# A gate builder copies eight tokens at a time out of PSUM, and the sample's second top-k becomes background work

## The chip, the cores and the metric

The kernel runs on one core of a Trainium2 chip. The metric is the time of one execution on the device, in microseconds; a kernel's figure is the median of several runs. Five engines work side by side: TensorE (PE in the profile, with PEld for its weight loads), VectorE (DVE), ScalarE (ACT), GpSimd (POOL), and SyncE (SP), which here only issues transfers. Each engine works through its own instructions strictly in the order in which the program was built.

## The reference

One layer of a decoder for 512 prompt tokens and a sample of 64 tokens: attention beside a short convolution, and then PEER, a mixture of 16384 experts of one neuron each. PEER is what the change touches:

```python
s = jnp.einsum('nhpc,hpkc->nhpk', q, sub_keys)
sv, si = lax.top_k(s, PEER_TOPK)                 # first top-k: 16 of 128 keys, for 2 halves of 8 heads
cand = sv[:, :, 0, :, None] + sv[:, :, 1, None, :]
cid = si[:, :, 0, :, None] * PEER_NKEYS + si[:, :, 1, None, :]
top, pos = lax.top_k(cand, PEER_TOPK)            # second top-k: 16 experts for each head
eid = jnp.take_along_axis(cid, pos, axis=-1)
g = jax.nn.softmax(top, axis=-1)
act = jax.nn.gelu(jnp.einsum('nd,nhkd->nhk', xf, u[eid]), approximate=False)
out = jnp.einsum('nhk,nhkd->nd', g * act, v[eid])
```

So each token takes 128 (expert, gate) pairs.

## The kernel before

The tokens lie in blocks of 128: block 0 to 3 are the prompt, block 4 is the sample (64 rows). PEER is computed in two ways.

**Gathered**, for block 0 and block 4: GpSimd fetches one row of u for each token and slot (`row`, L469, 512 KB), VectorE takes the dot product with the token (L477); later the same with rows of v, which VectorE adds up (`accg`, L484 and L487). These gathers are handed out a few at a time by `pump`, between other work, from a list `bg` of generators; `left` is the estimate of what remains, from which the pace of the last loop (`tail`) is set.

**Dense**, for blocks 1 to 3 (384 tokens): all 16384 experts are worked out for all tokens in 128 chunks of 128 experts. A *u-step* (`ustep`) loads a chunk of u (`ur`), splits it on ScalarE into a high part `uh` (L103) and on VectorE into a low part `ul` (L104), runs 24 matmuls of 384 columns into `pu`, and ScalarE writes `a` = gelu (L782). A *v-step* (`vprep`, `vmm`) multiplies `a` by the gates of this chunk (`w`, L898), splits, and runs 18 matmuls of 512 columns into the accumulators `y`. The u-steps of the first 68 chunks (LAG) may run ahead of everything; their results wait in DRAM (`Ad`) or in SBUF. The v-loop then takes chunks 68 to 127 first, each with its u-step, and after that chunks 0 to 67.

Between them stands the **gate build** (`gbuild`), which turns the 128 (expert, gate) pairs of every dense token into a full row of 16384 gates. For eight tokens at a time (TQ, called a *unit* here; 48 units in all) VectorE writes three one-hot tiles (L844, and L848 twice: `oj`, `oi`), ScalarE a fourth by eight scaled copies (`oi`, L852), TensorE multiplies them token by token into `pG`, and ScalarE copies `pG` into the staging tile `stg`. Four units fill one `stg`, which goes to DRAM (`Gd`, 12 stores of 2 MB); the v-steps read it back (`gt`). In `stg` the token is the innermost index ([expert row, 128, 32 tokens]), in `pG` it is the outer one:

```python
pg_ = psG.tile([P, 4, P], F32, name="pG")
...
nc.scalar.activation(stg[:, :, tl:tl + 4].rearrange("p i t -> p t i"), pg_, AF.Copy, scale=1.0 / GSC)
```

So this copy reads 512 consecutive words of PSUM and writes each of them 128 bytes behind the last.

A v-step needs gates of all 384 tokens, so the first v-step waits for the last store of `Gd`. The program's order on every engine is set at build time by a scheduler with its own estimate of costs; it moves u-steps, gathers and the pieces of a second top-k (`topk2`) to where it thinks their inputs are ready. The second top-k of the sample (`topk_gather` with st, 4, 64) is called behind the gate build, in one piece.

Of the kernel before, what the change touches and what calls it, by code (L numbers as in the profile page):

```python
# [9 lines left out]
F32 = mybir.dt.float32  # L10
# [5 lines left out]
AF = mybir.ActivationFunctionType  # L16
# [3 lines left out]
P = 128  # L20
# [10 lines left out]
SLOTS = 128  # L31
# [24 lines left out]
TQ = 8  # L56
NTB = ND // TB
GSC = 16384.0
# [9 lines left out]
def body(tc, I, O):  # L68
    nc = tc.nc
    top = ExitStack()  # L70

    def pool(stack, name, bufs=1, **kw):
        return stack.enter_context(tc.tile_pool(name=name, bufs=bufs, reuse_waits="tile", **kw))
# [369 lines left out]
    bg = []  # L443

    credit = [0.0]
    left = [0.0]
# [13 lines left out]
    def drain(gen):  # L460
        for _ in gen:
            pass

    def gather_units(k, nslot):
        idx, gat, x2, acc, av = idxg[k], gatg[k], x2g[k], accg[k], avg[k]

        def row(src, s):
            r = rows.tile([P, D], F32, name="row")
            nc.gpsimd.indirect_dma_start(out=r, out_offset=None, in_=I[src],  # L469
                                         in_offset=bass.IndirectOffsetOnAxis(ap=idx[:, s:s + 1], axis=0))  # L470
            return r

        for s in range(nslot):
            r = row("u", s)
            jk = keep2.tile([P, D], mybir.dt.bfloat16, name="jk2")
            tc.keep_in_program_order(
                nc.vector.tensor_tensor_reduce(jk, r, x2, 1.0, 0.0, OP.mult, OP.add, av[:, s:s + 1]))  # L477
            yield 1.135
        nc.scalar.activation(av[:, :nslot], av[:, :nslot], AF.Gelu)
        nc.vector.tensor_tensor(av[:, :nslot], av[:, :nslot], gat[:, :nslot], op=OP.mult)  # L480
        for s in range(nslot):
            r = row("v", s)
            if s == 0:
                tc.keep_in_program_order(nc.vector.tensor_scalar(acc, r, av[:, 0:1], None, op0=OP.mult))  # L484
            else:
                tc.keep_in_program_order(
                    nc.vector.scalar_tensor_tensor(acc, r, av[:, s:s + 1], acc, op0=OP.mult, op1=OP.add))  # L487
            yield 1.135
# [70 lines left out]
    def topk_gather(st, b, n, k):  # L559
        ef = tk.tile([P, SLOTS], F32, name="ef", bufs=2)  # L560
        if n == P:
            yield from topk2(st, b, n, ef, gatg[k])
            nc.vector.tensor_copy(idxg[k], ef)
            return
        gt = tk.tile([P, SLOTS], F32, name="gt", bufs=2)
        ei = tk.tile([P, SLOTS], I32, name="ei")
        yield from topk2(st, b, n, ef, gt)
        hs = SLOTS // 2
        nc.vector.tensor_copy(ei[:n], ef[:n])
        nc.vector.tensor_copy(idxg[k][:n, :hs], ef[:n, :hs])  # L570
        nc.vector.tensor_copy(gatg[k][:n, :hs], gt[:n, :hs])
        nc.sync.dma_start(idxg[k][n:2 * n, :hs], ei[:n, hs:])
        nc.sync.dma_start(gatg[k][n:2 * n, :hs], gt[:n, hs:])
        nc.sync.dma_start(x2g[k][n:2 * n, :], x2g[k][:n, :])
# [139 lines left out]
    def mkst(pl, grp):  # L714
        return {b: (pl.tile([P, 8, 2, 16], F32, name=f"sv{b}"), pl.tile([P, 8, 2, 16], U32, name=f"si{b}"))
                for b in grp}
# [37 lines left out]
    st = mkst(x2p, GB)  # L754
# [34 lines left out]
    def unext():  # L789
        if ui[0] < LAG:  # L790
            ustep(ui[0])
            ui[0] += 1
            pump(PUMP_WIN)
# [9 lines left out]
    psG = pool(gb_, "psG", bufs=2, space=PSUM)  # L803
# [8 lines left out]
    def gbuild(di, b):  # L812
        ef = tk.tile([P, SLOTS], F32, name="ef", bufs=2)
        gt = tk.tile([P, SLOTS], F32, name="gt", bufs=2)
        yield from topk2(st, b, P, ef, gt)
        ei = tk.tile([P, SLOTS], I32, name="ei")
        ii = tk.tile([P, SLOTS], I32, name="ii")
        ij = tk.tile([P, 2, SLOTS], F32, name="ij")
        nc.vector.tensor_copy(ei, ef)
        nc.vector.tensor_scalar(ii, ei, 7, None, op0=OP.logical_shift_right)  # L820
        nc.vector.tensor_copy(ij[:, 0, :], ii)
        nc.vector.tensor_scalar(ii, ei, 127, None, op0=OP.bitwise_and)
        nc.vector.tensor_copy(ij[:, 1, :], ii)
        pt = psG.tile([P, 4, P], F32, name="pT")
        nc.tensor.transpose(pt[:, 0, :], ij[:, 0, :], ident)
        nc.tensor.transpose(pt[:, 1, :], ij[:, 1, :], ident)
        nc.tensor.transpose(pt[:, 2, :], gt, ident)
        JT = gbp.tile([P, P], F16, name="JT")
        J4 = gbp.tile([P, 2, P, 4], F16, name="J4")
        gs = gbp.tile([P, P], F32, name="gs", bufs=1)  # L830
        gl = gbp.tile([P, P], F32, name="gl")
        nc.vector.tensor_copy(JT, pt[:, 1, :])
        nc.vector.tensor_copy(J4[:, 0], pt[:, 0, :].unsqueeze(2).to_broadcast([P, P, 4]))
        nc.vector.tensor_scalar(gs, pt[:, 2, :], GSC, None, op0=OP.mult)
        nc.vector.tensor_copy(J4[:, 1], gs.unsqueeze(2).to_broadcast([P, P, 4]))
        nc.vector.tensor_tensor(gl, gs, J4[:, 1, :, 0], op=OP.subtract)
        yield 1.5
        for tb in range(P // TB):
            stg = gbp.tile([P, NCH, TB], F32, name="stg")
            for q in range(TB // TQ):  # L840
                c0 = tb * TB + q * TQ
                cs = slice(c0, c0 + TQ)
                oj = gbp.tile([P, P, TQ], F16, name="oj")
                nc.vector.tensor_tensor(oj, iotaj, JT[:, cs].unsqueeze(1).to_broadcast([P, P, TQ]), op=OP.is_equal)  # L844
                OI = [gbp.tile([P, 32, TQ, 4], F16, name=f"oi{k}") for k in range(3)]
                f = "p a t b -> p a (t b)"
                for k, in0, op in ((0, iotax, OP.is_equal), (1, OI[0], OP.mult)):
                    nc.vector.tensor_tensor(OI[k].rearrange(f), in0.rearrange(f),  # L848
                                            J4[:, k, cs, :].rearrange("p t b -> p (t b)").unsqueeze(1)
                                            .to_broadcast([P, 32, TQ * 4]), op=op)  # L850
                for tt in range(TQ):
                    nc.scalar.activation(OI[2][:, :, tt, :], OI[0][:, :, tt, :], AF.Copy, scale=gl[:, c0 + tt:c0 + tt + 1])  # L852
                for q4 in range(TQ // 4):
                    pg_ = psG.tile([P, 4, P], F32, name="pG")
                    for t in range(4):
                        tt = q4 * 4 + t
                        nc.tensor.matmul(pg_[:, t, :], oj[:, :, tt], OI[1][:, :, tt, :], start=True, stop=False)
                        nc.tensor.matmul(pg_[:, t, :], oj[:, :, tt], OI[2][:, :, tt, :], start=False, stop=True)
                    tl = q * TQ + q4 * 4
                    nc.scalar.activation(stg[:, :, tl:tl + 4].rearrange("p i t -> p t i"), pg_, AF.Copy,  # L860
                                         scale=1.0 / GSC)
                yield 2.5
            nc.sync.dma_start(Gd[di * (P // TB) + tb], stg)

    debt = 0.0
    for di, b in enumerate(DENSE):
        for c in gbuild(di, b):
            debt += c
            while debt > WSTEP:
                unext()  # L870
                debt -= WSTEP
    while ui[0] < LAG:
        unext()
    drain(topk_gather(st, 4, 64, 1))
    bg.append(gather_units(1, SLOTS // 2))
    left[0] += SLOTS * 1.135
    gb_.close()

    vp = pool(top, "vp", bufs=2)
# [155 lines left out]
```

## Time and profile before

| | before |
|---|---|
| median of 3 runs | 1884.6 us (1877.14 to 1884.9) |
| span of the profiled execution, first to last instruction | 1882.2 us |
| PE busy in the span | 1738.2 us (92%) |
| DVE busy | 1430.9 us (76%) |
| ACT busy | 881.6 us (47%) |
| mean granted TensorE clock | 0.955 |
| moved by DMA | 533.75 MB, mean 284 GB/s |

The time listed for the runs is that of whole executions; the profile shows one execution, whose span lies 2.4 us below the median. Busy times are unions of the instructions' intervals; an instruction's own duration is longer than the step to the next one where the two overlap.

### The profile page before, as it was taken

Reading aid. Unit: us, or ns where it says so; the run is one execution under the profiler, and the core shown is the slowest. Engines: PE = TensorE matmul, PEld = TensorE weight load, DVE = VectorE, ACT = ScalarE, POOL = GpSimd, SP = SyncE. Lnnn points to the kernel's source line nnn. Section 1 sums busy time; section 2 is a strip of 40 time slices with the busy share of each in tenths; the row PEclk is TensorE's granted clock in tenths of the full one; section 3 lists DMA queues with packets and bytes.
Section 4 is the critical chain, followed back from the end, with each engine's and each line's share of the span. In section 5 each row is a group of like instructions: output and inputs, shape, how many; then the busy total and the mean of one; then the engine's idle time right before and its main releaser. Section 6 shows DMA issues by size and latency. Waiting matters only on the chain. (4 is left out here: it accounts for less than half of the span.)

```text
span 1882.2 us, 29066 instructions
## 1 busy us (share of the span) xinstructions
PE 1738.2 (92%) x10391; PEld 1467.3 (78%) x10391; DVE 1430.9 (76%) x3064; ACT 881.6 (47%) x1615; POOL 579.0 (31%) x483
## 2 busy tenths in 40 slices
PE   7999899997679999988988999999999999999997
PEld 5778655654558998987978889999999997777776
DVE  5433235766888999998788578888888778888888
ACT  4222366645323333479999933333333333333334
POOL 1010201014554214311212234544444444333330
PEclk9999979978788999999999999999999999999999
DMA  4257569858898448867777699999999999999996
GB/s 143 100 181 288 208 245 337 316 185 291 302 320 302 154 143 312 277 216 267 266 261 250 253 365 330 353 335 348 331 336 341 320 361 334 363 344 367 340 349 210
DMA packets 199077, 533.75 MB, mean 284 GB/s; under 512 B 17586, under 2 KB 82660, under 8 KB 197268
## 3 DMA queue, kind: packets, MB, share of 16 engines
q1 hardware_dynamic: 133364, 294.22, 44.0%
q0 software_dynamic: 65568, 237.69, 35.5%
q8 instruction: 81, 1.33, 0.3%
q14 instruction: 64, 0.52, 0.1%
HBM read 485.65 MB, written 45.63 MB: 282 GB/s over the span
## 5 line engine op out<-in xcount | busy, mean ns | idle before, releaser
L469 POOL DMA_INDIRECT row<-in_u,idxg x192 | 257.9, 1343 | 457.6 <-DVE avg L477 231.4
L469 POOL DMA_INDIRECT row<-in_v,idxg x192 | 264.5, 1377 | 421.6 <-DVE accg L487 345.3
L107 PE MATMUL pu<-x2h,uh 128*128 128x384 f32 x1024 | 350.9, 343 | 21.4 <-ACT a L782 11.1
L109 PE MATMUL pu<-x2h,ul 128*128 128x384 f32 x1024 | 352.0, 344 | 7.5 <-DVE ul L104 7.3
L108 PE MATMUL pu<-x2l,uh 128*128 128x384 f32 x1024 | 348.8, 341 | 0.0
L103 ACT ACTIVATE vh<-vr 128x1024 fp32r<-128x1024 f32 x128 | 135.8, 1061 | 290.4 <-PE y L913 251.4
L477 DVE CUSTOM_DVE_ANT_0 jk<-row,x2g 128x1024 bf16<-128x1024 f32 x192 | 233.8, 1218 | 28.0 <-DMA row<-in_u,idxg 26.8
L487 DVE SCALAR_TENSOR_TENSOR accg<-row,avg,accg 128x1024 f32<-128x1024 f32 x190 | 243.2, 1280 | 7.7 <-DMA row<-in_v,idxg 6.7
L909 PE MATMUL y<-vh,wh 128*128 128x512 f32 x768 | 224.7, 395 | 15.5 <-ACT wh L103 15.5
L911 PE MATMUL y<-vl,wh 128*128 128x512 f32 x768 | 234.2, 393 | 0.0
L107 PEld LDWEIGHTS pu<-x2h,uh 128*128 128x128 f32 x1024 | 196.5, 192 | 27.1 <-ACT a L782 12.2
L104 DVE TENSOR_TENSOR vl<-vr,vh 128x1024 fp32r<-128x1024 f32 x128 | 156.6, 1224 | 77.9 <-ACT vh L103 74.9
L913 PE MATMUL y<-vh,wl 128*128 128x512 f32 x768 | 215.6, 390 | 0.0
L109 PEld LDWEIGHTS pu<-x2h,ul 128*128 128x128 f32 x1024 | 196.4, 192 | 12.4 <-DVE ul L104 10.1
L103 ACT ACTIVATE uh<-ur 128x1024 fp32r<-128x1024 f32 x128 | 136.0, 1064 | 145.1 <-PE pu L108 74.1
L108 PEld LDWEIGHTS pu<-x2l,uh 128*128 128x128 f32 x1024 | 196.3, 192 | 1.7
L104 DVE TENSOR_TENSOR ul<-ur,uh 128x1024 fp32r<-128x1024 f32 x128 | 156.2, 1220 | 35.9 <-ACT uh L103 34.2
L909 PEld LDWEIGHTS y<-vh,wh 128*128 128x128 f32 x768 | 143.9, 189 | 46.5 <-ACT wh L103 19.5
L911 PEld LDWEIGHTS y<-vl,wh 128*128 128x128 f32 x768 | 145.1, 189 | 30.4
L913 PEld LDWEIGHTS y<-vh,wl 128*128 128x128 f32 x768 | 144.0, 188 | 30.1
L104 DVE TENSOR_TENSOR wlo<-wraw,whi 128x1024 fp32r<-128x1024 f32 (+1 forms) x96 | 91.0, 952 | 67.5 <-ACT whi L103 67.1
L103 ACT ACTIVATE whi<-wraw 128x1024 fp32r<-128x1024 f32 (+1 forms) x96 | 79.8, 840 | 124.3 <-PE mm L109 53.7
(281 smaller groups left out, 2936.4 us busy)
## 6 DMA issues: line engine op xcount, KB each, us to landing
ur<-in_ut SPq DMA_DIRECT2D x128, 512.0 KB
vr<-in_v SPq DMA_DIRECT2D x128, 512.0 KB
kt<-in_ck SPq DMA_DIRECT2D x60, 512.0 KB
vt<-in_cv POOLq DMA_DIRECT2D x60, 512.0 KB
Gd<-stg SPq DMA_DIRECT2D x12, 2048.0 KB
gt<-Gd SPq DMA_DIRECT2D x32, 768.0 KB
wraw<-in_w_in SPq DMA_DIRECT2D x24, 512.0 KB
Ad<-a SPq DMA_DIRECT2D x62, 192.0 KB
```

The source lines that it names most:

```text
L103: nc.scalar.activation(hi, src, AF.Copy)
L104: nc.vector.tensor_tensor(lo, src, hi.bitcast(F32), op=OP.subtract)
L107: nc.tensor.matmul(out, ah, bh, start=first, stop=False)
L108: nc.tensor.matmul(out, ah, bl, start=False, stop=False)
L109: nc.tensor.matmul(out, al, bh, start=False, stop=last)
L469: nc.gpsimd.indirect_dma_start(out=r, out_offset=None, in_=I[src], in_offset=bass.IndirectOffsetOnAxis(ap=idx[:, s:s + 1], axis=0))
L477: nc.vector.tensor_tensor_reduce(jk, r, x2, 1.0, 0.0, OP.mult, OP.add, av[:, s:s + 1]))
L487: nc.vector.scalar_tensor_tensor(acc, r, av[:, s:s + 1], acc, op0=OP.mult, op1=OP.add))
L909: nc.tensor.matmul(accs[b][k], wh[:, sl], vh[:, k * 512:k * 512 + 512], start=first, stop=False)
L911: nc.tensor.matmul(accs[b][k], wh[:, sl], vl[:, k * 512:k * 512 + 512], start=False, stop=False)
L913: nc.tensor.matmul(accs[b][k], wl[:, sl], vh[:, k * 512:k * 512 + 512], start=False, stop=last)
```

## The change

Two edits. In the gate build, `pG` holds eight tokens instead of four, all sixteen matmuls of a unit go into it, and one copy instead of two takes it to `stg`; the copy now runs along the tokens first, so that it writes 8 consecutive words and reads words that lie 512 bytes apart in PSUM. And the second top-k of the sample is put on the list `bg` behind block 0's gathers, ahead of the sample's own, instead of being written out in one piece; `left` grows by 24.

```diff
-                for q4 in range(TQ // 4):
-                    pg_ = psG.tile([P, 4, P], F32, name="pG")
-                    for t in range(4):
-                        tt = q4 * 4 + t
-                        nc.tensor.matmul(pg_[:, t, :], oj[:, :, tt], OI[1][:, :, tt, :], start=True, stop=False)
-                        nc.tensor.matmul(pg_[:, t, :], oj[:, :, tt], OI[2][:, :, tt, :], start=False, stop=True)
-                    tl = q * TQ + q4 * 4
-                    nc.scalar.activation(stg[:, :, tl:tl + 4].rearrange("p i t -> p t i"), pg_, AF.Copy,
-                                         scale=1.0 / GSC)
+                pg_ = psG.tile([P, TQ, P], F32, name="pG")
+                for tt in range(TQ):
+                    nc.tensor.matmul(pg_[:, tt, :], oj[:, :, tt], OI[1][:, :, tt, :], start=True, stop=False)
+                    nc.tensor.matmul(pg_[:, tt, :], oj[:, :, tt], OI[2][:, :, tt, :], start=False, stop=True)
+                nc.scalar.activation(stg[:, :, q * TQ:q * TQ + TQ], pg_.rearrange("p t i -> p i t"), AF.Copy,
+                                     scale=1.0 / GSC)
                 yield 2.5
...
-    drain(topk_gather(st, 4, 64, 1))
+    bg.append(topk_gather(st, 4, 64, 1))
     bg.append(gather_units(1, SLOTS // 2))
-    left[0] += SLOTS * 1.135
+    left[0] += SLOTS * 1.135 + 24.0
     gb_.close()
```

`pG` keeps two buffers, each now of two PSUM banks. The built order also differs. On ScalarE, the first units of the gate build before (L852 makes the fourth one-hot tile, L860 is the copy, L103 and L782 belong to a u-step):

```order
L852 ACTIVATE oi_7133<-oi_7131,gl 128x32x4 x8
L852 ACTIVATE oi_7168<-oi_7166,gl 128x32x4 x8
L103 ACTIVATE uh<-ur 128x1024
L782 ACTIVATE a<-pu 128x384
L860 ACTIVATE stg<-pG 128x4x128 x2
L852 ACTIVATE oi_7241<-oi_7239,gl 128x32x4 x8
L103 ACTIVATE uh<-ur 128x1024
L782 ACTIVATE a<-pu 128x384
L860 ACTIVATE stg<-pG 128x4x128 x2
```

and the same place in the changed kernel, where the copy is on L857:

```order
L852 ACTIVATE oi_7133<-oi_7131,gl 128x32x4 x8
L852 ACTIVATE oi_7166<-oi_7164,gl 128x32x4 x8
L103 ACTIVATE uh<-ur 128x1024
L782 ACTIVATE a<-pu 128x384
L857 ACTIVATE stg<-pG 128x128x8
L852 ACTIVATE oi_7237<-oi_7235,gl 128x32x4 x8
L857 ACTIVATE stg<-pG 128x128x8
L852 ACTIVATE oi_7270<-oi_7268,gl 128x32x4 x8
L103 ACTIVATE uh<-ur 128x1024
L782 ACTIVATE a<-pu 128x384
L857 ACTIVATE stg<-pG 128x128x8
```

Now some units stand without a u-step between them. Counted along TensorE's order, 38.0 u-steps (912 matmuls into `pu`) stood between the first and the last matmul into `pG`, and 31.9 do now; 31.1 stand ahead of the first in both. On ScalarE, from the last copy of the gate build on, before (`vh`, `wh` and `w` belong to the first v-steps):

```order
L860 ACTIVATE stg<-pG 128x4x128 x2
L103 ACTIVATE uh<-ur 128x1024
L782 ACTIVATE a<-pu 128x384
L103 ACTIVATE uh<-ur 128x1024
L782 ACTIVATE a<-pu 128x384
L103 ACTIVATE uh<-ur 128x1024
L103 ACTIVATE vh<-vr 128x1024
L103 ACTIVATE wh<-w 128x384
```

and in the changed kernel:

```order
L857 ACTIVATE stg<-pG 128x128x8
L103 ACTIVATE uh<-ur 128x1024 x2
L782 ACTIVATE a_11169<-pu 128x384
L782 ACTIVATE a_11205<-pu 128x384
L103 ACTIVATE uh<-ur 128x1024
L782 ACTIVATE a_11238<-pu 128x384
L103 ACTIVATE uh<-ur 128x1024
L103 ACTIVATE vh<-vr 128x1024
L782 ACTIVATE a_11274<-pu 128x384
L103 ACTIVATE vh<-vr 128x1024
L782 ACTIVATE a_11310<-pu 128x384
```

More u-steps stand between the last copy and the first v-step: along TensorE's order 7.1 instead of 3.9, and the first matmul into `y` has 70.1 u-steps ahead of it instead of 73.0. Last, on VectorE, the end of the sample's second top-k before (`ef`, `ei` and `idxg` are its results, 64 rows):

```order
L848 TENSOR_TENSOR oi_10270<-iotax,J_9608 128x1024
L556 CAST ef<-oh 64x8x8
L104 TENSOR_TENSOR ul<-ur,uh 128x1024
L569 CAST ei<-ef 64x128
L570 CAST idxg_5203<-ef 64x64
L848 TENSOR_TENSOR oi_10271<-oi_10270,J_9608 128x1024
L844 TENSOR_TENSOR oj<-iotaj,JT 128x1024
```

and in the changed kernel:

```order
L556 CAST ef<-oh 64x8x8
L848 TENSOR_TENSOR oi_10080<-iotax,J_9544 128x1024
L569 CAST ei<-ef 64x128
L570 CAST idxg_5203<-ef 64x64
L104 TENSOR_TENSOR ul<-ur,uh 128x1024
L477 ISA jk_10986,avg_2407<-row,x2g_2403 128x1024
L848 TENSOR_TENSOR oi_10081<-oi_10080,J_9544 128x1024
```

It stands among the units of the gate build in both kernels. Counted by the L844 rows ahead of it (one for each unit), its first piece stands at unit 13 before and 15 now, its last at unit 43 before and 41 now. Along the same order, between the first and the last L844, there were 39 `ul` of u-steps and 6 `accg` of v gathers, and there are 34 and 2 now. The last gather of all stands behind the 124th v-step's `vl` before and behind the 122nd now.

## Rows read from the trace of the kernel before

**Rows 1.** Windows by stage: us, busy us of each engine (instructions), granted clock, DMA share, GB/s

```profile
core 0: us, PE busy (x) PEld busy (x) DVE busy (x) ACT busy (x) POOL busy (x), PEclk, DMA share, GB/s
815.70:1076.90 261.20, 230.35 (x1685) 217.93 (x1684) 214.88 (x445) 253.04 (x551) 55.80 (x32) 0.94 0.72 256
1076.90:1094.80 17.90, 16.73 (x100) 16.41 (x98) 6.87 (x7) 7.61 (x11) 0.00 (x0) 1.00 0.93 339
1094.80:1570.00 475.20, 474.20 (x2382) 429.30 (x2382) 393.09 (x447) 169.45 (x230) 223.18 (x168) 1.00 0.95 340
1570.00:1870.00 300.00, 286.72 (x1240) 234.42 (x1241) 251.69 (x321) 108.01 (x144) 101.24 (x77) 0.99 0.95 339
```

**Rows 2.** Groups of ACT in the gate build: busy us, mean ns, idle before

```profile
L852 ACT ACTIVATE oi<-oi,gl 128x128 f16<-128x128 f16 x372 | 113.3, 415 | 0.0
L860 ACT ACTIVATE stg<-pG 128x512 f32<-128x512 f32 x94 | 99.1, 1163 | 5.0 <-PE pG L858 5.0
L103 ACT ACTIVATE uh<-ur 128x1024 fp32r<-128x1024 f32 x39 | 41.9, 1077 | 3.0 <-PE pu L108 1.9 <-DMA ur<-in_ut 1.1
```

**Rows 3.** Timeline of ACT in the gate build: start us, duration us, what

```profile
1022.39 2.48 ACT L852 ACTIVATE oi<-oi,gl 128x128 f16<-128x128 f16 x8
1024.71 0.53 ACT L782 ACTIVATE a<-pu 128x384 f32<-128x384 f32 x1
1025.08 2.16 ACT L860 ACTIVATE stg<-pG 128x512 f32<-128x512 f32 x2
1026.96 2.45 ACT L852 ACTIVATE oi<-oi,gl 128x128 f16<-128x128 f16 x8
1029.26 1.10 ACT L103 ACTIVATE uh<-ur 128x1024 fp32r<-128x1024 f32 x1
1030.21 2.10 ACT L860 ACTIVATE stg<-pG 128x512 f32<-128x512 f32 x2
```

**Rows 4.** Windows of the matmuls into `pu` alone, and into `pG`

```profile
815.70:1076.90 261.20, 183.17 (x914) 165.29 (x912) 19.23 (x39) 0.94 0.72 256
1076.90:1094.80 17.90, 16.57 (x94) 16.28 (x94) 1.13 (x4) 1.00 0.93 339
815.70:1076.90 261.20, 62.16 (x765) 99.12 (x94) 0.94 0.72 256
```

**Rows 5.** Timeline of PE: `pu` matmuls running free, and a half unit of `pG`

```profile
742.00 0.33 PE L109 MATMUL pu<-x2h,ul 128*128 128x384 f32 x1
...
746.16 0.33 PE L109 MATMUL pu<-x2h,ul 128*128 128x384 f32 x1
...
1032.36 0.22 PE L857 MATMUL pG<-oi,oj 128*128 128x128 f16 x1 [0.30 <-ACT stg L860]
...
1032.80 0.22 PE L858 MATMUL pG<-oi,oj 128*128 128x128 f16 x1
```

**Rows 6.** Waits in the gate build: us in total, times, longest

```profile
PEld L858 <- issue: 13.1, 18, 5.1
PE pG L857 <- ACT stg L860: 11.8, 15, 5.1
PE pu L107 <- ACT uh L103: 9.5, 8, 2.2
PE pu L107 <- ACT a L782: 7.3, 3, 2.8
```

**Rows 7.** ACT copies of other shapes, whole span

```profile
L222 ACT ACTIVATE PT<-pT 128x512 f32<-128x512 f32 x6 | 3.6, 593 | 2.8 <-PE pT L220 2.7
L222 ACT ACTIVATE PT<-pT 128x256 f32<-128x256 f32 x6 | 2.3, 376 | 3.4 <-PE pT L220 2.1 <-PE mm L228 1.3
L328 ACT ACTIVATE qbd<-pT 64x256 f32<-64x256 f32 x2 | 0.8, 378 | 1.7 <-PE pT L320 1.7
```

**Rows 8.** DVE groups with jumping writes, jumping reads, and neither

```profile
L515 DVE TENSOR_TENSOR cid<-sf 128x128 int16<-128x128 f32 x4 | 2.9, 724 | 0.0
L515 DVE TENSOR_TENSOR cand<-sv 128x128 f32<-128x128 f32 x4 | 1.1, 276 | 0.0
L531 DVE CAST tf<-tp 128x128 int16<-128x128 uint32 x4 | 1.2, 292 | 0.0
L563 DVE CAST idxg<-ef 128x128 int32<-128x128 f32 x1 | 0.2, 226 | 0.0
```

**Rows 9.** DVE groups in the gate build that belong to u-steps and to v gathers

```profile
L104 DVE TENSOR_TENSOR ul<-ur,uh 128x1024 fp32r<-128x1024 f32 x39 | 47.5, 1218 | 12.0 <-ACT uh L103 11.9
L487 DVE SCALAR_TENSOR_TENSOR accg<-row,avg,accg 128x1024 f32<-128x1024 f32 x6 | 7.7, 1277 | 0.0
```

## The prediction

> **What bounds the kernel now.** I read the windows by stage first, then, for the stage that the change is in, the groups of ScalarE, its timeline, the waits, and the matmuls.
>
> The windows [rows 1] cut the second half of the execution into four stages. From 815.7 to 1076.9 us is the gate build (261.2 us, first to last matmul into `pG`). ScalarE is busy 253.0 us of it, 97%. TensorE is busy 230.4 and VectorE 214.9, and the transfers take only 0.72 of the DMA engines. From 1094.8 to 1570 TensorE is busy 474.2 of 475.2 us: there nothing but matmuls counts. After 1570 it is still at 286.7 of 300, with DMA at 0.95. So TensorE bounds the kernel except in the gate build, and there ScalarE holds it up.
>
> What ScalarE does there is in its groups and its timeline [rows 2, 3]. Steps from one start to the next are what count when it is saturated: the fourth one-hot of a unit takes 1026.96 to 1029.26 = 2.30 us, two copies of `pG` 1025.08 to 1026.96 = 1.88, a split of `uh` 0.95, a gelu 0.37. A unit without a u-step is 4.18 us, 48 of them 200.6; 39 u-steps at 1.32 add 51.5; sum 252, which is what the window shows.
>
> How much work TensorE has there is not its busy time, since that counts overlapping intervals and slack between starts. Free running, 24 matmuls of a u-step take 742.00 to 746.16 = 4.16 us, and seven steps of `pG` matmuls 0.44, so 0.063 each [rows 5]. The gate build holds 914 matmuls into `pu`, 38.1 u-steps [rows 4]: 38.1 x 4.16 + 768 x 0.063 = 207 us of work in 261, and so 54 us lost. The waits say to whom: 11.8 us for `stg`, 9.5 for `uh`, 7.3 for `a`, all ScalarE, and 13.1 at its own sequencer [rows 6]. In the 17.9 us up to the first v-step, 94 matmuls (3.9 u-steps, 16.3 us) leave 1.6 us lost. Together 56 us, and this sum is what the change can shrink: every matmul has to run either way, and the stages behind are full.
>
> **The change part by part.** *The copy.* Per unit, two copies (a step of 1.88 us) become one of 1024 words. Its new shape is not in the trace. Below, it cannot be cheaper than a copy of 1024 words without jumps: `uh`, a step of 0.95 and 1077 ns long [rows 2, 3]. Above, the jump may cost on the read side what it costs now on the write side: today's copy of 512 words takes 1163 ns, where other copies of 512 words out of PSUM, without jumps, take 593 [rows 2, 7]; that would be 1.88 us for 1024 words, nothing gained. A jumping 2-byte write on VectorE even takes 724 ns against 276 [rows 8], 2.6 times, which would make 2.5 us.
>
> That writing 8 words in a row is free is shown: `qbd` is written in runs of 8 words with gaps, and its 256 words take 378 ns, those of a plain copy 376 [rows 7]. For jumping reads the nearest row is VectorE's `tf`, which reads words 64 bytes apart: 292 ns for 128, against 226 for a plain cast of 128 [rows 8]; the 66 ns more are 0.5 ns a word, far from the 448 more of the jumping write. It is another engine and another memory, but it is the nearest, so I take the lower end, 0.95 us. That takes 48 x 0.93 = 44.6 us from ScalarE.
>
> [...]
>
> *The u-steps.* The built order puts 31.9 u-steps instead of 38.0 among the units. ScalarE loses 6.1 x 1.32 = 8.1 us there, VectorE 5 `ul` at 1.22 and 4 `accg` at 1.28 [rows 9], 11.2 us. TensorE's work in the gate build falls by 25.4 to 181 us, but these 25.4 us come back behind it, where TensorE is full: about 3.2 u-steps before the first v-step (7.1 instead of 3.9, 29.5 us, which more than cover the 17.9 us to it, so the 1.6 us lost there go) and 2.9 in the stage at 474 of 475 us. This is why a shorter gate build alone is no gain: it must shrink by more than 25 us.
>
> *The length of the gate build.* ScalarE needs 253.0 - 44.6 - 8.1 = 200 us, VectorE 214.9 - 11.2 = 204, TensorE 181. Three engines in fixed orders, within 13% of each other. Today the bound engine loses 3% (253 in 261) with the next one at 85% of it; with the next at 98% each will often wait for the other. If the loss stayed 3%, the build would take 210 us; if it were 20%, 245. I choose 12%, between the two and nearer the middle, since VectorE already shows 12.0 us of waiting for `uh` while it is not the bound [rows 9]: 228 us. TensorE then loses 228 - 181 = 47 us instead of 56: **9 us gained**. At 210 us it loses 29, a gain of 27; at 245 it loses 64, 8 us more than now.
>
> *`pG` in two tiles of eight tokens.* A copy now waits for 16 matmuls (1.0 us) instead of 8, hidden behind the eight scaled copies of the next unit, which stand ahead of it (2.30 us). Without that cover it would be 0.5 us a unit, 24 us. TensorE may run a whole unit further ahead; that works on the 11.8 us, and is inside the choice above.
>
> *The top-k of the sample.* The scheduler had already spread it among the units, and does so now, from unit 15 to 41 instead of 13 to 43. Nothing moves to another stage, and I cost it at nothing; what hides it is that it stands in VectorE's 204 us in both. The 24 in `left` quickens the gathers a little; the last one goes from behind the 124th `vl` to the 122nd, so none is exposed at the end. Bytes are the same, and with DMA at 0.95 in both last stages no gain is to be had there either.
>
> Sum against the profiled execution: 1882.2 - 9 = 1873.2 us, and with the 2.4 us by which the median lies above it, 1875.6.
>
> **The rivals.** *The jump is paid on the read (slower).* At 1.88 us a copy ScalarE needs 200 + 48 x 0.93 = 245 us, at its 3% 253. TensorE then loses 253 - 181 = 72 us, 16 more than now: 1900.6. The decider is the copy's step: above about 1.57 us (ScalarE at 230 us, a build of 237) the change loses. For it speaks that the write jump costs a factor of two on this engine; against it `tf`. At 2.5 us a copy it would be 46 us more, near 1930.
>
> *The engines mesh (a larger gain).* With the 3% loss, 210 us, it comes to 1857.6. For it: PE's waits for ScalarE all shrink, and two deep `pG` buffers decouple the units. Against: VectorE is level with ScalarE.
>
> *VectorE takes over (no change).* It does its 204 us in an order in which top-k pieces, gathers and one-hots compete; at a build of 240 to 250 us the time is 1888 to 1898. For it: the 12.0 us for `uh`. Against: two thirds of its work are one-hots and splits whose inputs come early.
>
> **How the numbers follow.** The likeliest case (build of 215 to 240 us, 1862 to 1888) gets 0.50, half of it faster than 1875.2, which is 0.5% under the median (about what a measurement of this kernel can tell from no change). The larger gain gets 0.13, VectorE taking over 0.12 (two thirds of it within 0.5%), the paid read 0.20, and 0.05 is for a dearer read. Faster: 0.26 + 0.13 and a little, 0.40. Within 0.5%: 0.24 + 0.08 + 0.03, 0.35. Slower: 0.17 + 0.04 + 0.04, 0.25. The range takes in the paid read and leaves out the best of the gains: 1860 to 1902; the likeliest case's own is 1862 to 1888.
>
> **What would show it.** The copy, with 128x1024 words, at about 1060 ns (right) or near 2000 (the rival). The window of the gate build near 228 us, with ScalarE and VectorE both near 200 busy in it and TensorE's matmuls into `pu` at some 766. More `pu` matmuls between the gate build and the first v-step (170 instead of 94), and the stage from there to the last u-step some 12 us longer, still full. I am wrong if the build is under 215 us or over 240 with a cheap copy, or if the last stage changes its length by more than a few microseconds.

## The result

The changed kernel is slower: 1894.3 us (median of 7 runs, 1887.7 to 1899.7) against 1883.2 (7 runs of the kernel before beside them), a ratio of 1.006, 95% interval 1.0036 to 1.0083.

The windows by stage, cut as in [rows 1] (gate build; up to the first v-step; u-steps and v-steps; v-steps alone), of the changed kernel:

```profile
822.00:1047.20 225.20, 207.49 (x1540) 191.66 (x1539) 205.22 (x440) 204.85 (x499) 52.26 (x28) 0.95 0.76 273
1047.20:1088.70 41.50, 35.17 (x176) 33.71 (x175) 16.76 (x16) 13.56 (x19) 5.24 (x4) 0.88 0.83 304
1088.70:1575.80 487.10, 486.03 (x2453) 441.17 (x2452) 389.49 (x442) 171.42 (x232) 224.96 (x166) 1.00 0.91 326
1575.80:1885.70 309.90, 287.61 (x1244) 233.29 (x1243) 255.38 (x327) 107.82 (x147) 101.14 (x80) 0.99 0.95 334
```

The last two stages of the kernel before, cut at the same events ([rows 1] cut them at 1570):

```profile
1094.80:1568.60 473.80, 473.72 (x2381) 429.14 (x2382) 392.13 (x445) 168.14 (x229) 221.85 (x168) 1.00 0.95 340
1568.60:1870.10 301.50, 287.30 (x1244) 234.64 (x1243) 252.75 (x323) 109.39 (x147) 102.56 (x78) 0.99 0.95 339
```

The gate build fell from 261.2 to 225.2 us, 36.0 less. Behind it everything grew: 41.5 us to the first v-step instead of 17.9 (23.6 more), 487.1 to the last matmul into `pu` instead of 473.8 (13.3 more), 309.9 of v-steps alone instead of 301.5 (8.4 more). That is 9.3 us lost, near the 11 us between the medians. The two profiled spans lie 15.6 us apart (1897.8 and 1882.2); 6.6 of these arose before the first u-step, which none of the edits touch.

The groups of ScalarE in the gate build, to hold against [rows 2]:

```profile
L852 ACT ACTIVATE oi<-oi,gl 128x128 f16<-128x128 f16 x380 | 116.1, 399 | 0.6 <-DVE oi L848 0.6
L857 ACT ACTIVATE stg<-pG 128x1024 f32<-128x1024 f32 x47 | 47.9, 1020 | 7.6 <-PE pG L856 7.4
L103 ACT ACTIVATE uh<-ur 128x1024 fp32r<-128x1024 f32 x32 | 33.8, 1056 | 7.2 <-DMA ur<-in_ut 6.9 <-PE pu L108 0.2
```

The copy is as cheap as one without jumps (`uh`, also 1024 words, takes 1056 ns): 1024 words in 1020 ns, 47.9 us in all instead of 99.1, though every read jumps 512 bytes. The matmuls into `pu`, first in the gate build, then behind it up to the first v-step, to hold against [rows 4]:

```profile
822.00:1047.20 225.20, 159.00 (x768) 139.38 (x767) 15.93 (x33) 0.95 0.76 273
1047.20:1088.70 41.50, 35.01 (x170) 33.50 (x170) 2.92 (x7) 0.88 0.83 304
```

768 and 170 of them, 32.0 and 7.1 u-steps, as the built order said. The 7.1 u-steps are 29.5 us of work, so 12.0 of the 41.5 us are lost. The waits of that stretch name the cause:

```profile
DVE ul L104 <- ACT uh L103: 16.2, 5, 6.0
ACT uh L103 <- DMA ur<-in_ut: 6.5, 3, 3.6
PE pu L107 <- ACT uh L103: 5.4, 2, 4.3
```

ScalarE waits for rows of u that have not landed, and TensorE waits behind it. The loads of u, from issue to landing (the last number, us), first in the last 47 us of the gate build and then in the hand-over, from 1047 to 1075 us:

```profile
ur<-in_ut SPq DMA_DIRECT2D x7, 512.0 KB, 5.0
ur<-in_ut SPq DMA_DIRECT2D x4, 512.0 KB, 8.7
```

And the windows around the longest wait:

```profile
1060.00:1072.00 12.00, 10.24 (x49) 9.80 (x48) 7.11 (x6) 4.99 (x6) 3.36 (x2) 0.86 1.08 391
1072.00:1077.00 5.00, 0.68 (x3) 0.40 (x2) 0.42 (x1) 1.81 (x3) 0.00 (x0) 0.94 1.03 420
1077.00:1081.00 4.00, 3.75 (x12) 3.24 (x12) 2.03 (x2) 0.79 (x1) 0.00 (x0) 0.50 0.65 189
```

The DMA engines are full there (391 and 420 GB/s, shares of 1.08 and 1.03): loads of u compete with the first loads of v and of the gates, which in part were issued ahead of them (v from 1054.4 us and gates from 1058.8, before the next u at 1067.0). How much each of the two, the shared engines and the order of issue, adds was not tested. Behind the wait of 4.3 us the granted clock is 0.50, and one matmul into `pu` starts 0.32 us after the last, against 0.17 running free [rows 5]. In the whole stretch TensorE was idle for 41.5 - 35.2 = 6.3 us, and its 29.5 us of work took 35.2; so of the 12.0 us lost about half is idle time and the rest slower work, where the granted clock is 0.88 instead of 1.00.

Last, the gathers. GpSimd's timeline (start us, duration us, in brackets the idle time before) in the middle of the third stage:

```profile
1417.46 0.94 POOL L469 DMA_INDIRECT row<-in_u,idxg  x1 [0.30 <-issue]
1423.22 0.94 POOL L469 DMA_INDIRECT row<-in_u,idxg  x1 [4.82 <-DVE avg L477]
1465.41 1.75 POOL L469 DMA_INDIRECT row<-in_u,idxg  x1 [41.26 <-DVE avg L477]
1468.23 1.01 POOL L469 DMA_INDIRECT row<-in_u,idxg  x1 [1.07 <-DVE avg L477]
```

For 42 us no gather is issued, since VectorE's next dot product stands that far behind in its order. The windows around it (same columns as above):

```profile
1380.00:1420.00 40.00, 40.00 (x203) 36.25 (x202) 33.78 (x37) 14.78 (x21) 22.12 (x15) 1.00 0.98 356
1420.00:1465.00 45.00, 45.00 (x232) 41.28 (x232) 20.49 (x24) 16.42 (x23) 0.94 (x1) 1.00 0.56 185
```

Transfers fall from 356 to 185 GB/s for 45 us, some 7.7 MB that have to be moved later. TensorE, full in this stage, does not notice. Most of it is caught up within the stage: in the last stage, where transfers were at 0.95 already, 80 gathers fall instead of 78 (the count at POOL), two more of 512 KB. In the kernel before, the longest pause behind the first v-step is 8.5 us.

### The profile page after: what moved, and what is told of

Same layout as the page of the kernel before. It is cut to its first block, busy times and chain, and to the rows that moved or that the text cites. A ratio compares the mean times of both kernels' runs of the same rounds, so it can differ in the third digit from the quotient of the medians.

```text
span 1897.8 us, 28948 instructions
## 1 busy us (share of the span) xinstructions
PE 1751.8 (92%) x10391; PEld 1470.7 (77%) x10391; DVE 1428.7 (75%) x3064; ACT 838.9 (44%) x1567; POOL 585.4 (31%) x483
## 5 line engine op out<-in xcount | busy, mean ns | idle before, releaser
L469 POOL DMA_INDIRECT row<-in_u,idxg x192 | 273.7, 1426 | 476.5 <-DVE avg L477 237.8
L469 POOL DMA_INDIRECT row<-in_v,idxg x192 | 255.0, 1328 | 394.6 <-DVE accg L487 324.0
L103 ACT ACTIVATE vh<-vr 128x1024 fp32r<-128x1024 f32 x128 | 135.8, 1061 | 326.0 <-PE y L910 263.6
L906 PE MATMUL y<-vh,wh 128*128 128x512 f32 x768 | 230.5, 394 | 22.3 <-ACT wh L103 22.3
L107 PEld LDWEIGHTS pu<-x2h,uh 128*128 128x128 f32 x1024 | 197.5, 193 | 23.6 <-ACT uh L103 11.8
L103 ACT ACTIVATE uh<-ur 128x1024 fp32r<-128x1024 f32 x128 | 135.2, 1057 | 135.2 <-DMA ur<-in_ut 60.0
L104 DVE TENSOR_TENSOR wlo<-wraw,whi 128x1024 fp32r<-128x1024 f32 (+1 forms) x96 | 91.0, 952 | 70.1 <-ACT whi L103 69.2
L103 ACT ACTIVATE whi<-wraw 128x1024 fp32r<-128x1024 f32 (+1 forms) x96 | 79.9, 841 | 126.8 <-PE mm L109 53.5
```

Source lines behind the costliest of these rows:

```text
L103: nc.scalar.activation(hi, src, AF.Copy)
L104: nc.vector.tensor_tensor(lo, src, hi.bitcast(F32), op=OP.subtract)
L107: nc.tensor.matmul(out, ah, bh, start=first, stop=False)
L906: nc.tensor.matmul(accs[b][k], wh[:, sl], vh[:, k * 512:k * 512 + 512], start=first, stop=False)
```

## The experiments

Three suspects: **A**, the pause in the gathers, from the second edit; **B**, the u-steps that moved out of the gate build and the stall at the hand-over, from the first; later **C**, that what moves them is the depth of `pG`, and not the copy. Ratios are to the kernel before, run on the same chip beside each; medians of two experiments can come from different chips, on which the kernel before took 1882.3 to 1885.5 us, and then the ratios are compared.

**copy_only**: the first edit alone.

```diff
-    bg.append(topk_gather(st, 4, 64, 1))
+    drain(topk_gather(st, 4, 64, 1))
     bg.append(gather_units(1, SLOTS // 2))
-    left[0] += SLOTS * 1.135 + 24.0
+    left[0] += SLOTS * 1.135
```

> The first edit alone: one copy of eight tokens, the sample's second top-k written out in one piece as before. Theory A (the gathers pause): the changed kernel lost its time because the paced list pays for pieces of the top-k that had already been placed, so that no gather is handed out for 42 us in the middle of the dense stages, and some 7 MB of gathers move into the last stage. Then here no gap between gathers over 15 us stands behind the first v-step, the stage of v-steps alone falls from 309.9 back to about 302 us, and the time is 6 to 10 us under the changed kernel: a ratio to the kernel before of 0.999 to 1.002. Theory B (the u-steps moved out and the hand-over stalls): the loss comes from the first edit, by the 41.5 us between the gate build and the first v-step; then the ratio stays at 1.005 to 1.006.

Measured: 1883.0 us, ratio 0.998 (0.9963 to 0.9997). Its windows, all but the gate build (222.2 us):

```profile
1037.40:1078.70 41.30, 35.05 (x176) 33.59 (x175) 16.67 (x16) 13.48 (x19) 5.23 (x4) 0.88 0.83 305
1078.70:1564.10 485.40, 485.40 (x2453) 441.43 (x2452) 395.25 (x448) 169.34 (x231) 228.99 (x169) 1.00 0.93 329
1564.10:1867.10 303.00, 287.79 (x1244) 234.59 (x1243) 250.51 (x321) 108.79 (x147) 100.36 (x77) 0.99 0.94 338
```

No pause, and the last stage is back at 303.0. The ratio lies just under the range of A, and B's is ruled out: the second edit makes the loss against the kernel before. But the hand-over is 41.3 us here too, and copies that are together some 45 us cheaper have gained 3 to 4 us: B holds for where the gain went.

**topk_only**: the second edit alone, on the kernel before.

```diff
-    drain(topk_gather(st, 4, 64, 1))
+    bg.append(topk_gather(st, 4, 64, 1))
     bg.append(gather_units(1, SLOTS // 2))
-    left[0] += SLOTS * 1.135
+    left[0] += SLOTS * 1.135 + 24.0
```

> The second edit alone, with the two copies of four tokens as before. In the built order the hole without gathers is five split steps long here and ten in the changed kernel. Theory A: a pause of about 20 us in the gathers, 3 MB moved to the last stage, 3 to 5 us slower than before: ratio 1.001 to 1.003. Theory B: nothing moves, 1.000.

Measured: 1888.9 us, ratio 1.0018 (1.0001 to 1.0035). Its pause, and its last two stages:

```profile
1451.81 1.01 POOL L469 DMA_INDIRECT row<-in_u,idxg  x1 [0.60 <-DVE avg L477]
1472.11 1.94 POOL L469 DMA_INDIRECT row<-in_u,idxg  x1 [19.29 <-DVE avg L477]
```
```profile
1108.80:1582.70 473.90, 473.78 (x2381) 429.18 (x2382) 388.18 (x439) 168.72 (x229) 224.31 (x165) 1.00 0.93 336
1582.70:1892.00 309.30, 288.06 (x1244) 233.02 (x1243) 255.11 (x329) 108.41 (x146) 104.73 (x81) 0.99 0.94 337
```

The third stage is that of before to a tenth (473.9 us); the last is 7.8 us longer. The edit costs where A says. The pause is half as long as in the changed kernel, and the last stage nearly as long, so the cost is not in proportion to the pause. Nor did 3 MB move: 81 gathers fall in the last stage instead of 78, three more, 1.6 MB.

**narrow_new_walk**: the kernel before, with nothing but the copy's walk changed.

```diff
-                    nc.scalar.activation(stg[:, :, tl:tl + 4].rearrange("p i t -> p t i"), pg_, AF.Copy,
+                    nc.scalar.activation(stg[:, :, tl:tl + 4], pg_.rearrange("p t i -> p i t"), AF.Copy,
```

> The kernel before with nothing changed but the walk of the copy: two copies of four tokens each, but running along the tokens first, so that 4 words in a row are written. The built order is that of the kernel before, with 38 u-steps among the units. If the write jump was the price, the copy takes about 0.56 to 0.60 us instead of 1.16; if fewer and larger copies were the gain, it stays near 1.16. With a cheap copy ScalarE needs 253 - 42 = 211 us; both theories then expect a gate build of 232 to 240 us instead of 261 with TensorE's full 207 us of work in it, and no later loss: ratio 0.986 to 0.991.

Measured: **1854.7 us, ratio 0.984 (0.9827 to 0.9857)**, the fastest kernel of this study. The copy, and the four stages:

```profile
L860 ACT ACTIVATE stg<-pG 128x512 f32<-128x512 f32 x95 | 51.8, 596 | 4.0 <-PE pG L858 4.0
```
```profile
818.80:1049.80 231.00, 219.02 (x1685) 208.12 (x1684) 215.12 (x450) 216.78 (x558) 80.59 (x32) 0.99 0.81 292
1049.80:1066.60 16.80, 16.74 (x100) 16.42 (x98) 6.74 (x7) 6.40 (x10) 0.00 (x0) 1.00 0.89 324
1066.60:1540.50 473.90, 473.73 (x2381) 429.15 (x2382) 392.05 (x446) 168.28 (x229) 221.26 (x168) 1.00 0.95 340
1540.50:1841.20 300.70, 286.25 (x1244) 233.38 (x1243) 252.51 (x323) 109.51 (x147) 101.68 (x78) 0.99 0.95 340
```

Four words in a row are enough: 596 ns, as a plain copy with its 593 [rows 7]. The order is that of before, with 38 u-steps in the gate build, which takes 231.0 us, a little less than expected, and nothing comes back behind it. The 30.2 us there are nearly the whole gain. The granted clock in the gate build rose with it, from 0.94 to 0.99.

**copy_lag64**: the first edit, and a v-loop that may start four u-steps earlier.

```diff
-LAG = 68
+LAG = 64
```

> The first edit alone with LAG at 64 instead of 68, so that the v-loop may start four u-steps earlier: the first v-step has 67.8 u-steps ahead of it instead of 70.1, with the same 63.0 at the end of the gate build. Theory B (the hand-over costs): the stretch from the gate build to the first v-step shrinks from 41.5 to 22 to 28 us, and the time falls by the idle part of it, 5 to 10 us under copy_only. Theory A: what is lost lies in the gathers, and this equals copy_only within 3 us.

Measured: 1876.4 us, ratio 0.9956 (0.9941 to 0.9971), 6.6 under copy_only. Its hand-over holds 4.8 u-steps (20.0 us):

```profile
1038.00:1060.50 22.50, 20.64 (x120) 19.99 (x119) 10.56 (x12) 9.51 (x13) 1.95 (x2) 1.00 0.96 341
```

2.5 us are lost in it instead of 12, at the full clock. As B expected; but one can take back no more than this stall this way.

**after_free**: the changed kernel, with the top-k still on the list but charged at nothing.

```diff
-    bg.append(topk_gather(st, 4, 64, 1))
+    bg.append(0.0 for _ in topk_gather(st, 4, 64, 1))
     bg.append(gather_units(1, SLOTS // 2))
-    left[0] += SLOTS * 1.135 + 24.0
+    left[0] += SLOTS * 1.135
```

> The changed kernel, with the sample's top-k still on the background list, but its pieces charged at nothing there and left as before. Theory A in its narrow form (the pause comes from the pace paying for pieces that the scheduler has long placed): no pause over 15 us behind the first v-step, v-steps alone back to 301 to 304 us, time as copy_only: ratio 0.997 to 1.000. Theory A in its wide form (the place on the list itself, a dependence or a later start of the sample's gathers): the 42 us pause stays, ratio 1.004 to 1.007.

Measured: 1884.3 us, ratio 1.002 (0.9998 to 1.0043). Its longest wait for a dot product from 1090 us to the last v-step (total, times, longest), and its last stage:

```profile
POOL row L469 <- DVE avg L477: 97.5, 44, 8.6
```
```profile
1563.00:1869.50 306.50, 287.68 (x1244) 233.24 (x1244) 251.84 (x321) 108.89 (x147) 99.75 (x76) 0.99 0.94 332
```

No pause is left behind the first v-step, so it is the charge that makes it, and not the place on the list. The time came back only in part and missed the range of the narrow form: v-steps alone took 306.5 us, where copy_only had 303.0 with the same number of gathers (308) issued by its start. The other 3.5 us stay unexplained; wide_old_walk below, without a pause, took 305.7.

This run also drops the 24 in `left`, which quickens the pace of all gathers, and no run separates the two. The trace shows that this pace has a price of its own. The last 20 us of the v-steps, before, changed, and here:

```profile
1850.10:1870.10 20.00, 20.00 (x90) 16.57 (x89) 17.97 (x31) 9.78 (x16) 0.00 (x0) 1.00 0.46 141
1865.70:1885.70 20.00, 20.00 (x90) 16.57 (x89) 14.77 (x26) 8.61 (x14) 0.00 (x0) 1.00 0.28 93
1849.60:1869.60 20.00, 20.00 (x90) 16.56 (x89) 18.04 (x30) 9.77 (x16) 0.00 (x0) 1.00 0.44 135
```

With the 24 the last gather comes two v-steps earlier, and about 1 MB less is moved in these 20 us, so that it falls into the part of the stage where the DMA engines are full (0.95 over the whole stage); topk_only and narrow_topk show the same (92 and 91 GB/s). Together with the two or three gathers that come from the third stage this is 2 to 2.5 MB, 6 to 7.5 us at 339 GB/s: an estimate that accounts for the longer last stage, without telling how it is shared between the pause and the pace.

**wide_old_walk**: one copy of eight tokens, in the walk of before.

```diff
-                nc.scalar.activation(stg[:, :, q * TQ:q * TQ + TQ], pg_.rearrange("p t i -> p i t"), AF.Copy,
+                nc.scalar.activation(stg[:, :, q * TQ:q * TQ + TQ].rearrange("p i t -> p t i"), pg_, AF.Copy,
```

With the top-k in one piece, as in copy_only.

> One copy of eight tokens in the old walk: it reads 1024 words in a row and writes each 128 bytes behind the last. If the write jump is the price, 1024 words take 1.9 to 2.1 us, twice today's 512, and the gate build, with 31.9 u-steps, takes 250 to 260 us. If the gain came from one instruction in place of two, it takes about 1.1 us.

Measured, one run: 1921.4 us, a gate build of 252.5 us; the copies, min/median/max:

```profile
L857 ACT ACTIVATE stg<-pG x48: 1921/2098/2222, 822.5 to 1074.5; 128x1024 f32<-128x1024 f32 x48
```

2098 ns against 1020 for the same 1024 words: the write jump is the whole price, and merging two copies gains nothing by itself.

**narrow_topk**: narrow_new_walk and the second edit, as in topk_only:

```diff
-    drain(topk_gather(st, 4, 64, 1))
+    bg.append(topk_gather(st, 4, 64, 1))
-    left[0] += SLOTS * 1.135
+    left[0] += SLOTS * 1.135 + 24.0
```

> The copy of four tokens with the new walk, and the second edit on top. The built order has the same hole of five split steps as with the second edit alone. Theory A: a pause of about 20 us in the gathers, v-steps alone 5 to 8 us longer than the 300.7 of narrow_new_walk, and 2 to 6 us more than its 1854.7: ratio 0.985 to 0.988. Theory B (the second edit costs nothing): 0.984.

Measured: 1859.5 us, ratio 0.9889 (0.986 to 0.9919), 4.8 us over narrow_new_walk by the medians and 9 by the ratios, a little over the expected range. A pause of 19.28 us, and again the last stage alone is longer, by 7.3 us:

```profile
1060.40:1534.60 474.20, 474.02 (x2380) 429.11 (x2381) 388.34 (x440) 168.44 (x229) 222.09 (x165) 1.00 0.93 336
1534.60:1842.60 308.00, 288.87 (x1244) 234.51 (x1244) 255.40 (x329) 108.17 (x146) 104.52 (x81) 0.99 0.94 338
```

**narrow_lag66**: narrow_new_walk with a v-loop that may start two u-steps earlier. Against narrow_new_walk:

```diff
-LAG = 68
+LAG = 66
```

> The copy of four tokens with the new walk, LAG at 66: two u-steps instead of 3.9 stand between the gate build and the first v-step. If about 17 us of latency (last store of the gates, first load back) have to be covered by u-steps there, TensorE idles some 8 us: hand-over still 16 to 18 us with 2 u-steps in it, and the time is 3 to 8 us over narrow_new_walk, less some 2 us that two fewer round trips of a through DRAM give back: ratio 0.985 to 0.988. If the latency is not what holds the first v-step, the hand-over shrinks to 8 to 10 us and the ratio is 0.982 to 0.984.

Measured: 1870.2 us, ratio 0.9929 (0.9907 to 0.995), 15.5 us over narrow_new_walk by the medians and 16 by the ratios, twice what was expected. The hand-over is the predicted one, 16.5 us with 51 matmuls in it and a granted clock of 0.86:

```profile
1047.30:1063.80 16.50, 8.23 (x51) 7.91 (x49) 5.54 (x6) 4.61 (x7) 0.00 (x0) 0.86 0.88 321
```

So some 17 us pass between the last gates and the first v-step with two u-steps as with 3.9 (16.5 and 16.8 us), and 3.9 u-steps fill them. TensorE's wait before the first v-step explains 8 of the 15 us. Of the others 1.7 lie in the gate build (232.7 us) and 5.4 in the last two stages (492.7 and 295.6 us, 13.7 more, of which 8.3 are the two u-steps that moved there); their cause stays open. The 2 us put down to fewer round trips of `a` were an estimate that no run shows by itself.

**narrow_deep4** and **wide_one_buf**: why did the u-steps move? The first is narrow_new_walk with four buffers of `pG`, the second copy_only with one.

```diff
-                    pg_ = psG.tile([P, 4, P], F32, name="pG")
+                    pg_ = psG.tile([P, 4, P], F32, name="pG", bufs=4)
```
```diff
-                pg_ = psG.tile([P, TQ, P], F32, name="pG")
+                pg_ = psG.tile([P, TQ, P], F32, name="pG", bufs=1)
```

> The copy of four tokens with the new walk, and four buffers for pG instead of two, the same PSUM as two buffers of eight tokens. The built order then has 31.9 u-steps among the units and 7.1 between them and the first v-step, as with the first edit. Theory C (the depth of pG, and not the size of the copy, moves the u-steps out, and their moving costs the gain): gate build 218 to 226 us, hand-over 38 to 44 us, the U+V stage 485 us, time as copy_only: ratio 0.996 to 1.000. Theory D (the eight-token copy itself costs it): as narrow_new_walk, 0.983 to 0.986.

> The first edit alone with one buffer of eight tokens for pG instead of two, the same PSUM as before. The built order has 37.0 u-steps among the units and 4.8 behind them. Theory C: the u-steps stay in, so the gain of the copy shows: hand-over 18 to 24 us, U+V stage 474 to 478 us, gate build 232 to 245 us (TensorE waits for each copy before the next unit): ratio 0.984 to 0.991. Theory D: as copy_only, 0.996 to 1.000.

Measured: narrow_deep4 1874.6 us, ratio 0.9937 (0.9916 to 0.9959); wide_one_buf 1864.5, ratio 0.9897 (0.9868 to 0.9926). The gate build and the hand-over of each:

```profile
825.40:1037.90 212.50, 201.12 (x1539) 184.60 (x1538) 201.24 (x435) 204.63 (x539) 90.72 (x28) 0.98 0.80 288
1037.90:1079.40 41.50, 32.94 (x176) 31.47 (x175) 17.89 (x17) 13.77 (x20) 5.24 (x4) 0.92 0.83 304
```
```profile
822.20:1055.60 233.40, 217.25 (x1661) 206.15 (x1660) 213.05 (x444) 212.01 (x503) 70.25 (x32) 0.98 0.79 283
1055.60:1076.90 21.30, 20.57 (x121) 19.94 (x120) 10.82 (x13) 8.90 (x13) 1.01 (x1) 1.00 1.01 361
```

C holds in both directions: deeper buffers alone bring the 41.5 us hand-over to the narrow copy, and cost it 18 us by the ratios; a single buffer takes the hand-over from the wide copy, and gains it 16. The first came out some 4 us faster than the low end expected, by a build of 212.5 us instead of 218 to 226.

## Why the prediction was wrong

It forecast 1875.6 us, faster; the kernel is slower, 1894.3. That this time lies between 1860 and 1902 is luck: the upper end stood for a paid read, which did not come. By its steps:

- *What bounds the kernel.* Right. ScalarE held up the gate build, and relieving it alone gave 30.2 us (narrow_new_walk), a little over half of the 54 us that TensorE lost there.
- *The copy.* Right. 0.95 us was taken for a step; the copy is 1020 ns long. The jump is paid on the write alone: 2098 ns for 1024 words written 128 bytes apart (wide_old_walk), 1020 ns for 1024 words read 512 bytes apart out of PSUM. The nearest row, VectorE's `tf`, pointed the right way.
- *The length of the gate build.* Right: 228 forecast, 225.2 measured, ScalarE 204.9 and VectorE 205.2 busy. TensorE loses 225.2 - 181 = 44 us there instead of 54. The 12% that led to it was chosen between 3 and 20, and 10% came out.
- *The u-steps.* Half right. The 2.9 that come back in the third stage cost what was said (12 us forecast, 13.3 measured). The step that failed is "29.5 us, which more than cover the 17.9 us to it, so the 1.6 us lost there go". It counted work and latency, but not that the loads of u for those steps compete with the first loads of gates and of v, nor the lower clock behind a wait (0.50 from 1077 to 1081 us): 12.0 us were lost there instead of none. This alone ate the 10 us of the gate build; copy_only, without the second edit, stands at 0.998.
- *The top-k of the sample.* The other step that failed, and the one that made the kernel slower: "Nothing moves to another stage, and I cost it at nothing". The pieces of the top-k had not moved, but the pace still paid for them. The yields of `topk2` add up to 19.0; a v-step with its u-step hands out about 2.8 gathers of 1.135, some 3.2, and so the gathers would stop for about six such steps, 8.2 us each, some 49 us; 42 were measured. The same sum does not fit topk_only and narrow_topk, where the charge is the same and the pause 19.3 us; what halves it there was not found. The prediction had looked at the first and the last gather in the built order, not at the distance between two neighbours, which shows the hole before any run. Two or three gathers moved to the last stage. The prediction also took it for harmless that the gathers end two v-steps earlier; this leaves the DMA engines at 0.28 in the last 20 us of a stage that stands at 0.95. The second edit costs 7 to 8 us of the last stage wherever it appears (309.9, 309.3 and 308.0 against 303.0, 301.5 and 300.7, each beside the same kernel without it); how much of that is the pause and how much the pace stays open.
- *The rivals.* None of the three came true. The sign was that of the first rival, its mechanism was not. Of the signs of being wrong that were named, the last stage's 8.4 us is the one that showed.

Against the forecast the build was 2.8 us shorter, the hand-over 12.0 longer (41.5 instead of 29.5), the third stage 1.2 and the last one 8.4 longer: 18.8 us, nearly all of what lies between 9 gained and 9.3 lost.

How much the moved u-steps cost in all was priced only as work that comes back. narrow_deep4 against narrow_new_walk shows it: 18.5 us gained in the build, 24.7 lost at the hand-over and 11.4 in the third stage, so 17.6 lost in all; 18 by the ratios.

## What to carry to other kernels

Here a ScalarE copy of 512 words out of PSUM took 596 ns when it read with jumps of 512 bytes and wrote four words in a row, and 1163 when it read in a row and wrote each word 128 bytes behind the last. Change such a walk first, alone, and keep tile sizes and buffer counts, since a deeper buffer lets a scheduler reorder work far from the edit (narrow_deep4: a hand-over of 41.5 us instead of 16.8). Work that is put on a paced list must not be charged there if it is placed elsewhere, or what stands behind it on the list pauses (42 us here); and a pace that ends background transfers early leaves the DMA engines partly idle at the end (0.28 in the last 20 us, instead of 0.46). In a built order, compare the largest distance between neighbours of a stream, not only its ends.

## What the runs showed of the hardware

- ScalarE read PSUM words 512 bytes apart at no extra cost (1020 ns for 1024 words, with 1056 for `uh`, which reads SBUF and does not jump), while writes 128 bytes apart in SBUF took twice as long (2098 ns). Writes in runs of four words cost no more than unbroken ones (596 and 593 ns for 512 words).
- The first u-step's first matmul starts between 663.7 and 682.0 us in the twelve profiled executions, though the edits stand behind it. A single time is therefore uncertain by about 1%, and the lengths of stages tell more than spans: the third stage of the four kernels with 38 u-steps in the gate build and LAG at 68 was 473.8, 473.9, 473.9 and 474.2 us long.
- After a wait of 4.3 us TensorE ran at a granted clock of 0.50 from 1077 to 1081 us of the changed kernel, with 0.32 us from one matmul into `pu` to the next; over the hand-over of 41.5 us the clock was 0.88, and the stretch lost 12.0 us with 6.3 us of idle time.
